# Hybrid gated-conv and forgetting-attention block: where four pairs of decay rows are issued, and when two rows of squares are taken

## The chip, the cores and the metric

The kernel runs on one core of one Trainium2 chip. The metric is the device time of one execution in microseconds, the median of several runs. TensorE is called PE here (its weight loads PEld), VectorE DVE, ScalarE ACT, GpSimd POOL and SyncE SP.

## The reference

One trunk layer over 512 positions of width 1024, all in float32, cut to what matters here:

```python
h = rms_norm(x, norm_mix_g)
cb, cc, cin, q, k, v, f_logit, g_logit = split(h @ w_in)
y_conv = (cb * causal_dwconv(cc * cin)) @ w_out_conv
F = cumsum(log_sigmoid(f_logit + b_f))                  # decay, one row per head
s = q.k / sqrt(64) + F[t] - F[s]                        # s <= t, 8 heads of 64
y_attn = softmax(s) @ v @ w_out_attn
x = x + (sigmoid(g_conv) * y_conv + sigmoid(g_attn) * y_attn) @ w_o
a, b = split(causal_dwconv(rms_norm(x, norm_ffn_g) @ w_up))   # 2 x 2816
x = x + (silu(a) * b) @ w_down
out = x * rsqrt(mean(x * x, -1) + 1e-6) * norm_f_g
```

## The kernel before

Everything is held transposed: features on the 128 partitions, the 512 positions along the free axis, so `x1` is eight rows of blocks (`x1[:, m, :]`, m = 0 to 7). Each float32 product is made of three matmuls on a high and a low half: a weight chunk arrives by DMA as `raw`, ACT copies it to the high half `wh` (L259), DVE subtracts to get the low half `wl` (L263), and PE multiplies high by high, low by high and high by low. This splitting is the work that PE always waits for, if it waits. The tiles `wh` and `wl` have two buffers each, `raw` has four (two to four for the forms below); SP issues the weight loads in the order of one list, `stream`, and each waits until the split has freed its buffer.

The program runs through stages: the projection of v, then q and k of the first two head pairs, then attention (32 units of one head and one block of 128 queries, with half a projection between two units as filler, L589 and L590 being the score matmuls), gates, mix, output projection, the up projection and the down projection.

**Decay rows.** The cumulated decay is in one tile `fr`, written once on DVE (L684). For every pair of heads `pr`, `evac_qk` evacuates q and k (`t_q`, `t_k`), copies and splits them on ACT (L531), POOL (L532) and DVE (L533), and `put_f` (L513) copies rows of `fr` by DMA into spare rows of the tiles `qb` and `kb`, two DMAs of 4 KB for q and two for k. Score matmul L590 multiplies `qb` by `kb` and so adds the decay. Pairs 0 and 1 use different `qb` and `kb` buffers; pairs 2 and 3 use them again. A score goes on to DVE (L594, minimum), ACT (L598, `pp`), POOL (L602, scaling) and back to PE, which transposes it (L618, `tp`) three units later.

**Down projection.** The function `seven` makes 2 by 2 blocks of it with seven products in place of eight. Its weights come as two chunks for each step, a plain one (`P`, three products for each block) and a formed one (`F`, four; sums of weights prepared in DRAM). Output rows are made in pairs i = 0 to 3, rows 2i and 2i + 1. In the second of the two phases pair 2 ends first, then pair 0, and then pair 1; pair 3's rows come at the very end by plain products. When a pair is done, `combine` puts its remaining additions (`z1` to `a4`, L1107 to L1126) into a list `later`; in phase 1 it adds two calls of `final_square` for the pair's two rows, which square a row on ACT (L1139 or L1142), add it to `ssq3` on DVE (L1143) and scale the row by the last norm's weight on ACT (L1144).

Work in `later` is done behind a weight split: `run_later(k, us)` goes through the list in order, takes each entry that is allowed from split `k` on while a budget of microseconds lasts, and stops at the first allowed entry that does not fit. The first number of an entry is the split from which it is allowed:

```python
if later[n][0] <= k and later[n][1] <= us + 0.1:
    us -= later[n][1]
    with after_split():
        later.pop(n)[3]()
elif later[n][0] <= k:
    return
```

PE's order is fixed by hand (`keep`). ACT, DVE and POOL orders outside `keep` come from the tile scheduler, which may move an instruction ahead of another.

Of the kernel before, what the change touches and what calls it, by code (L numbers as in the profile page):

```python
# [61 lines left out]
DOUBLES = GATES + STEPS[0] + STEPS[1]  # L62
# [4 lines left out]
def block_kernel(ctx, tc, xT, vecs, wv, win, wmix, wo, wup, wst, wdp, outT):  # L67
# [3 lines left out]
    nc = tc.nc  # L71
# [12 lines left out]
    def ring(*ids):  # L84
        st = [0]

        def f(name):
            st[0] += 1
            return bank(ids[(st[0] - 1) % len(ids)], name)

        return f
# [29 lines left out]
    stream = [(f"v{kb}", wv[kb], S + H) for kb in range(KB)]  # L121
# [247 lines left out]
    def ct(name):  # L369
        return ap.tile([P, S], F32, tag="ct", name=name, bufs=NCT)  # L370
# [109 lines left out]
    def proj(idx, name, evac, bank):  # L480
        st = {}

        def half(i):
            if i == 0:
                st["w"] = chunk(f"in{idx}")
                st["p"] = bank(f"p_{name}")
            wh, wl = st["w"]
            for kb in range(4 * i, 4 * i + 4):
                ks = slice(kb * P, (kb + 1) * P)
                mm3(st["p"], wh[:, ks], wl[:, ks], xgh[:, kb, :], xgl[:, kb, :], kb == 0, kb == KB - 1)  # L490
            if i == 1:

                while len(parts) < chunk.n + 2:
                    split()
                with after_split():
                    evac(st["p"])

        return [lambda: half(0), lambda: half(1)]
# [13 lines left out]
    def put_f(dst, f0, eng):  # L512
        eng.dma_start(dst.bitcast(F32), fr[f0 : f0 + H + 1 : H, :].bitcast(F32))  # L513

    def evac_qk(pr, isq):
        def f(p):
            nm = f"{'q' if isq else 'k'}{pr}"
            t = ct(f"t_{nm}")
            if isq:
                nc.vector.scalar_tensor_tensor(t, p, -(HD ** -0.5), rb1, op0=ALU.mult, op1=ALU.mult)  # L520
            else:
                nc.vector.tensor_mul(t, p, rb1)
            a = ap.tile([P, 2, S], F32R, tag="qt" if isq else "ka", name=f"a_{nm}", bufs=2)
            b = (QB if isq else KBt)[pr % 2]
            (QT if isq else KA)[pr] = a
            af = a.bitcast(F32)
            for e in range(2):
                own, other = slice(e * HD, (e + 1) * HD), slice((1 - e) * HD, (2 - e) * HD)
                second = (b[own, e, :], a[other, e, :])
                cp2, lo = second if isq else second[::-1]  # L530
                nc.scalar.activation(a[own, e, :], t[own, :], AF.Copy)  # L531
                nc.gpsimd.tensor_scalar(cp2, t[own, :], 1.0, 0.0, op0=ALU.mult, op1=ALU.add)  # L532
                nc.vector.tensor_sub(lo, t[own, :], af[own, e, :])  # L533
                f0 = 2 * pr + e + (2 * H if isq else 0)
                r = AUX[e] + (0 if isq else 2)
                put_f(b[r : r + 2, e, :], f0, nc.scalar if pr < 2 else nc.gpsimd)

        return f

# [127 lines left out]
    z, e, o = (ap.tile([n, S], F32, tag="pp", name=nm, bufs=NPP) for nm in ("fz", "fe", "fo"))  # L667
# [38 lines left out]
    f0, f1 = proj(12, "q0", st.append, ring(7))  # L706
# [21 lines left out]
    for idx in late:  # L728
        kind, i = divmod(idx, 4)
# [9 lines left out]
    for i in range(n + LA):  # L739
# [8 lines left out]
        if 0 <= i - LA < n:  # L748
            pr, e, qb = units[i - LA]
# [95 lines left out]
    def x_sums(qs):  # L845
        b11, b12, b21, b22 = (xq[:, qs, i, :] for i in range(4))

        def f():
            nc.vector.tensor_sub(b11, b11, b12)
            nc.vector.tensor_sub(b12, b22, b12)  # L850

        def g():
            nc.vector.scalar_tensor_tensor(b22, b11, -1.0, b22, op0=ALU.mult, op1=ALU.subtract)
            nc.vector.scalar_tensor_tensor(b21, b22, -1.0, b21, op0=ALU.mult, op1=ALU.subtract)

        return f, g
# [9 lines left out]
    for q in (0, 2):  # L866
        f, g = x_sums(slice(q, q + 2))
# [56 lines left out]
    for j in range(KB):  # L924
# [20 lines left out]
        a, b = gs  # L945
# [153 lines left out]
    def combine(ph, i, banks, ids):  # L1099

        m1, m2 = x1[:, 2 * i, :], x1[:, 2 * i + 1, :]
        p23, p45, p16, p7 = banks[0], banks[1], banks[2], banks[3][:, th[0]]
        t = {}

        def z1():
            t["z"] = fp.tile([P, S], F32, tag="fz", name=f"cz{ph}{i}", bufs=2)
            nc.scalar.activation(t["z"][:, th[0]], p16[:, th[0]], AF.Copy)  # L1107
            nc.vector.tensor_add(t["z"][:, th[1]], p16[:, th[1]], t["z"][:, th[0]])

        def a1():  # L1110
            nc.vector.tensor_add(m1, p23, m1)

        def u3():
            t["u"] = fp.tile([P, S], F32, tag="fz", name=f"cu{ph}{i}", bufs=2)[:, : 2 * P]
            nc.vector.tensor_add(t["u"], p7, t["z"][:, th[1]])
            nc.vector.tensor_add(m1[:, th[1]], p45[:, th[1]], m1[:, th[1]])

        def a2():
            nc.vector.tensor_sub(m2, m2, p45)

        def a3():
            nc.vector.tensor_add(m1, m1, t["z"])

        def a4():
            m2h = m2.rearrange(halves_of, h=2)
            nc.vector.tensor_sub(m2h, m2h, t["u"].unsqueeze(1).to_broadcast([P, 2, 2 * P]))  # L1126

        for f, us, x in ((z1, 0.42, 2), (a1, 0.7, 0), (u3, 0.85, 3), (a2, 0.7, 1), (a3, 0.7, None), (a4, 0.7, None)):
            later.append((0, us, () if x is None else ids if x == 3 else (ids[x],), f))
        if ph == 1:  # L1130
            first = [c[0] for c in stream].index(f"F{len(DOUBLES) - 2}") if i == 0 else 0
            for m in (2 * i, 2 * i + 1):
                later.append((first, 0.8, (), lambda m=m: final_square(m)))

    def final_square(m):
        y = x1[:, m, :]
        if final_square.first:
            final_square.first = False
            nc.scalar.activation(ssq3, y, AF.Square)  # L1139
        else:  # L1140
            sq = fp.tile([P, S], F32, tag="fu", name=f"sq3_{m}", bufs=3)
            nc.scalar.activation(sq, y, AF.Square)  # L1142
            nc.vector.tensor_add(ssq3, ssq3, sq)  # L1143
        nc.scalar.activation(y, y, AF.Copy, scale=col(GF + m))  # L1144
# [3 lines left out]
    for ph, (j0, j1) in enumerate(PHASES):  # L1148
        if ph:
            flush()  # L1150
            acc = ring(*X)
        if ph:
            make_forms(len(GATES) + len(STEPS[0]), len(DOUBLES), ph)
        for j in range(j0, j1):
            pu = None
            if j == 0:
                nrm = {}

                def mid():
                    nrm["c"] = rstd_col([ssq2], NT, 6, "n2")  # L1160

                def late():
                    nrm["b"] = rstd_sb(rstd_bc(nrm["c"], NT, 7, "n2"), "n2")

                pu = lead(["up0", "up1"], x1h, x1l, mid, late)
            glu(ph, j, up(j, nrm["b"], pu))
        assert not todo_bg
        seven(
            STEPS[ph], len(GATES) + ph * len(STEPS[0]), ({0: X, 1: Y, 3: X, 2: Y}, {0: X, 1: Y, 2: Y})[ph],
            lambda q, g: (gh[:, place(ph, q) + g, :], gl[:, place(ph, q) + g, :]),  # L1170
            goes_on=HELD if ph == 1 else None, stays=HELD if ph == 0 else None,
            done=lambda i, banks, ids: combine(ph, i, banks, ids),
        )
# [190 lines left out]
```

## Time and profile before

| | |
|---|---|
| median of 3 runs | 701.56 us (701.47 to 701.98) |
| profiled execution | 702.08 us |
| its span | 700.0 us |
| mean granted PE clock | 0.997 |
| PE busy | 690.9 us, 99% of the span |
| DVE, ACT, POOL busy | 501.7, 344.0, 171.5 us |

The profiled execution is 0.52 us above the median and 2.08 us longer than its span, which runs from the first to the last instruction. In rows of a timeline the first number is the start in us from the span's start, the second the length (of the whole group for "x2"), and the brackets hold the idle time before it and what ended it. ACTq, SPq and POOLq are an engine's queue issuing a DMA. Consecutive matmuls overlap: their start to start is what counts, not the length of one.

### The profile page before, as it was taken

What the parts mean: (1) busy time and instruction counts of PE and PEld (TensorE: products, weight loads), DVE (VectorE), ACT (ScalarE), POOL (GpSimd) and SP (SyncE); (2) the same over time, 40 slices, a digit from 0 to 9 for tenths busy, and PEclk for the clock granted to TensorE, in tenths of its full rate; (3) what the DMA queues carried; (4) which work ended last, traced back from release to release, by engine and by line L of the source; (5) the groups of instructions that cost most, each with busy time, mean ns of one, the idle gap of its engine ahead of it and who ended that gap; (6) DMA issues with size and microseconds to landing.
All of it is one profiled execution on the core that took longest, in us unless ns stands there. A gap on an engine that the chain in (4) does not pass through costs nothing. (4 is left out here: it accounts for less than half of the span.)

```text
span 700.0 us, 14606 instructions
## 1 busy us (share of the span) xinstructions
PE 690.9 (99%) x6008; PEld 689.2 (98%) x6008; DVE 501.7 (72%) x783; ACT 344.0 (49%) x546; POOL 171.5 (24%) x187
## 2 busy tenths in 40 slices
PE   9999999999999999999999999999999999999996
PEld 9999999999999999999999999999999999999995
DVE  6678877776678778754377777778774677877783
ACT  5574655645565444543344444445443345545563
POOL 4124846532100000224504214110000322311001
PEclk9999999999999999999999999999999999999998
DMA  7527978542452555586977855545546686676413
GB/s 251 155 85 255 210 186 196 124 91 89 149 172 80 179 185 178 182 298 150 216 192 169 218 121 129 157 159 176 194 132 223 146 190 158 182 185 166 147 31 121
DMA packets 52578, 116.02 MB, mean 166 GB/s; under 512 B 4848, under 2 KB 23296, under 8 KB 52512
## 3 DMA queue, kind: packets, MB, share of 16 engines
q1 hardware_dynamic: 37456, 94.16, 41.3%
q0 software_dynamic: 13792, 19.72, 17.4%
q10 hardware_dynamic: 1264, 1.22, 0.5%
q8 instruction: 47, 0.77, 0.4%
q14 instruction: 19, 0.16, 0.1%
HBM read 112.92 MB, written 33.03 MB: 208 GB/s over the span
## 5 line engine op out<-in xcount | busy, mean ns | idle before, releaser
L290 PE MATMUL p_up<-x1h,wh_up 128*128 128x256 f32 x536 | 104.5, 276 | 0.0
L290 PE MATMUL p_up<-x1h,wl_up 128*128 128x256 f32 x536 | 104.4, 276 | 0.0
L290 PE MATMUL p_up<-x1l,wh_up 128*128 128x256 f32 x536 | 104.3, 276 | 0.0
L259 ACT ACTIVATE wh_up<-raw_up 128x1024 fp32r<-128x1024 f32 x44 | 46.7, 1060 | 86.8 <-PE p_up L290 73.4
L290 PEld LDWEIGHTS p_up<-x1h,wl_up 128*128 128x128 f32 x536 | 80.7, 188 | 0.0
L290 PEld LDWEIGHTS p_up<-x1h,wh_up 128*128 128x128 f32 x536 | 80.7, 188 | 0.0
L290 PEld LDWEIGHTS p_up<-x1l,wh_up 128*128 128x128 f32 x536 | 80.6, 188 | 0.0
L263 DVE TENSOR_TENSOR wl_up<-raw_up,wh_up 128x1024 fp32r<-128x1024 f32 x44 | 53.8, 1223 | 20.6 <-ACT wh_up L259 20.6
L290 PE MATMUL p_in<-xgh,wl_in 128*128 128x256 f32 x288 | 56.7, 278 | 0.1
L290 PE MATMUL p_in<-xgh,wh_in 128*128 128x256 f32 x288 | 56.8, 279 | 0.0
L1061 POOL TENSOR_TENSOR ge<-fu,fu 128x512 f32<-128x512 f32 x11 | 17.1, 1550 | 161.6 <-DVE fu L547 150.9
L290 PE MATMUL p_in<-xgl,wh_in 128*128 128x256 f32 x288 | 56.5, 278 | 0.0
L201 POOL DMA_DIRECT2D f<-in_wst_dram x48 | 55.9, 1285 | 0.0
L1046 DVE TENSOR_TENSOR fz<-p_up,rb_n 128x512 f32<-128x512 f32 x44 | 30.3, 690 | 31.6 <-PE p_up L290 31.6
L263 DVE TENSOR_TENSOR wl_F<-raw_F,wh_F 128x1024 fp32r<-128x1024 f32 (+1 forms) x30 | 40.4, 1346 | 14.3 <-ACT wh_F L259 14.3
L259 ACT ACTIVATE wh_F<-raw_F 128x1024 fp32r<-128x1024 f32 (+1 forms) x30 | 31.5, 1051 | 28.8 <-PE dn L308 25.8
L290 PEld LDWEIGHTS p_in<-xgh,wh_in 128*128 128x128 f32 x288 | 44.7, 188 | 0.7
L290 PEld LDWEIGHTS p_in<-xgh,wl_in 128*128 128x128 f32 x288 | 43.6, 188 | 0.3 <-DVE wl_in L263 0.3
L290 PEld LDWEIGHTS p_in<-xgl,wh_in 128*128 128x128 f32 x288 | 43.7, 188 | 0.0
L308 PE MATMUL p_up<-x1h,wh_up 128*128 128x256 f32 x168 | 40.3, 277 | 0.0
L308 PE MATMUL p_up<-x1l,wh_up 128*128 128x256 f32 x168 | 40.2, 276 | 0.0
L263 DVE TENSOR_TENSOR wl_in<-raw_in,wh_in 128x1024 fp32r<-128x1024 f32 x26 | 34.6, 1332 | 7.1 <-ACT wh_in L259 6.9
(318 smaller groups left out, 2038.4 us busy)
## 6 DMA issues: line engine op xcount, KB each, us to landing
raw_up<-in_wup_dram SPq DMA_DIRECT2D x44, 512.0 KB, 4.9
raw_F<-f SPq DMA_DIRECT2D x29, 512.0 KB, 4.0
raw_in<-in_win_dram SPq DMA_DIRECT2D x26, 512.0 KB, 3.6
raw_P<-in_wst_dram SPq DMA_DIRECT2D x29, 384.0 KB, 3.7
f<-in_wst_dram POOLq DMA_DIRECT2D x29, 256.0 KB, 5.6
f<-in_wst_dram SPq DMA_DIRECT2D x14, 512.0 KB, 5.8
f<-in_wst_dram POOLq DMA_DIRECT2D x14, 512.0 KB, 8.0
f<-f SPq DMA_DIRECT2D x28, 256.0 KB, 5.0
```

Source lines behind the costliest of these rows:

```text
L201: return lambda: keep(nc.gpsimd.dma_start(dst, src, accum_op=ALU.add))
L259: ins = nc.scalar.activation(hi, raw, AF.Copy)
L263: ins = nc.vector.tensor_sub(lo, raw, hi.bitcast(F32))
L290: keep(nc.tensor.matmul(out[:, cs], w, x[:, cs], start=start and i == 0 and c == 0, stop=stop and i == 2 and c == len(cut) - 1,))
L308: keep(nc.tensor.matmul(out, wl if x == 1 else wh, xl if x == 2 else xh, start=opens and bk not in seen, stop=closes and bk not in left,))
L1046: nc.vector.tensor_mul(z, p, rb2)
L1061: keep(nc.gpsimd.tensor_mul(ge, a.rearrange(halves_of, h=2), b.rearrange(halves_of, h=2)))
```

## The change

Two edits. In `evac_qk` the DMAs of the decay rows get other queues: before, pairs 0 and 1 were on ACT and pairs 2 and 3 on POOL; now pair 0's q is on ACT, pair 0's k on SP, and pairs 1, 2 and 3 on POOL. In `combine` the two `final_square` calls of pair 2 are allowed only from the split of the last but one `F` chunk on, as those of pair 0 were before; those of pair 1 are allowed at once, as before.

```diff
@@ evac_qk
                 r = AUX[e] + (0 if isq else 2)
-                put_f(b[r : r + 2, e, :], f0, nc.scalar if pr < 2 else nc.gpsimd)
+                put_f(b[r : r + 2, e, :], f0, nc.gpsimd if pr else nc.scalar if isq else nc.sync)
@@ combine
         if ph == 1:
-            first = [c[0] for c in stream].index(f"F{len(DOUBLES) - 2}") if i == 0 else 0
+            first = [c[0] for c in stream].index(f"F{len(DOUBLES) - 2}") if i != 1 else 0
             for m in (2 * i, 2 * i + 1):
                 later.append((first, 0.8, (), lambda m=m: final_square(m)))
```

In the rows below a name ends in its buffer's number; `-` is before, `+` after. On ACT, where q and k of the first two pairs are evacuated (`qb_109` and `kb_111` are pair 0's, `qb_110` and `kb_112` pair 1's; `wh_in_708` is the first attention filler's weight):

```order
 L531 ACTIVATE a_k_648<-t_k_646 64x512 x2
 L513 DMA qb_109<-fr 2x512 x2
-L513 DMA kb_111<-fr 2x512 x2
 L259 ACTIVATE wh_in_708<-raw_in_453 128x1024
-L513 DMA qb_110<-fr 2x512 x2
+L531 ACTIVATE a_q_714<-t_q_712 64x512 x2
 L259 ACTIVATE wh_in_774<-raw_in_556 128x1024
-L531 ACTIVATE a_q_714<-t_q_712 64x512 x2
-L513 DMA kb_112<-fr 2x512 x2
 L598 ACTIVATE pp_800,m_798<-s_795,m_798 128x128
```

Six of the eight DMAs leave ACT, and pair 1's copies of q (`a_q_714`) move ahead of one weight split. Two of the six go to SP, between the weight loads `raw_in_624` and `raw_in_706`; the four of pair 1 go to POOL:

```order
 L532 TENSOR_SCALAR a_k_648<-t_k_646 64x512 x2
+L513 DMA qb_110<-fr 2x512 x2
+L513 DMA kb_112<-fr 2x512 x2
 L532 TENSOR_SCALAR qb_110<-t_q_712 64x512 x2
 L532 TENSOR_SCALAR a_k_780<-t_k_778 64x512 x2
```

On POOL they stand behind pair 0's copies and ahead of pair 1's. On DVE, at the same place, the two subtractions of `a_q_714` (L533) move ahead of the first score's minimum (`s_795`) and of the split `wl_in_775`.

On ACT near the end of the down projection (`wh_F_8496` of before is `wh_F_8494` now, `wh_P_8527` is `wh_P_8524`; `cz` is pair 0's `z1`; the row ahead of these is the split `wh_P_8466` in both):

```order
+L1107 ACTIVATE cz_8470<-dn_8257 128x256
+L259 ACTIVATE wh_F_8494<-raw_F_8309 128x1024
 L1139 ACTIVATE ssq_4484<-x_3960 128x512
-L1142 ACTIVATE sq_5_8472<-x_3960 128x512
-L1144 ACTIVATE x_3960<-x_3960,vec 128x512 x2
-L259 ACTIVATE wh_F_8496<-raw_F_8309 128x1024
-L1107 ACTIVATE cz_8500<-dn_8257 128x256
-L259 ACTIVATE wh_P_8527<-raw_P_8337 128x768
+L1144 ACTIVATE x_3960<-x_3960,vec 128x512
+L259 ACTIVATE wh_P_8524<-raw_P_8337 128x768
+L1142 ACTIVATE sq_5_8528<-x_3960 128x512
+L1144 ACTIVATE x_3960<-x_3960,vec 128x512
```

The squares and scalings of pair 2 leave the place ahead of the formed weight's split; one row of them now stands between that split and the next plain one, the other behind that. On DVE pair 0's first two additions (L1108, L1111) move ahead of the formed weight's `wl`, and the addition of `sq_5` (L1143) behind the next plain weight's `wl`. PE's instructions and their order are the same.

## The prediction

> **What bounds the kernel now.** First the page's busy times, then who PE and its weight loads waited for:
>
> ```profile
> PE 690.9 (99%) x6008; PEld 689.2 (98%) x6008; DVE 501.7 (72%) x783; ACT 344.0 (49%) x546; POOL 171.5 (24%) x187
> ```
> ```profile
> PE dn L308 <- ACT wh_F L259: 0.9, 1, 0.9
> ```
> ```profile
> PEld p_in L290 <- DVE wl_in L263: 0.3, 1, 0.3
> ```
>
> PE is the bound and its instructions don't change, so only its holes can be won. Behind its start the view of waits lists these two by name: 0.9 us for a formed weight's split on ACT, 0.3 us for a filler weight's low half on DVE. The change touches just those two places. The timeline of PE gives what each costs from start to start:
>
> ```profile
> 653.53 0.84 PE L308 MATMUL dn<-gh,wl_P 128*128 128x256 f32 x6
> ...
> 658.97 0.28 PE L308 MATMUL dn<-gh,wh_F 128*128 128x256 f32 x1
> ...
> 665.63 0.84 PE L308 MATMUL dn<-gh,wl_P 128*128 128x256 f32 x6
> 667.35 0.38 PE L308 MATMUL dn<-gh,wh_F 128*128 128x256 f32 x1 [0.88 <-ACT wh_F L259]
> ...
> 672.40 0.28 PE L308 MATMUL dn<-gh,wh_F 128*128 128x256 f32 x1
> ```
>
> Six low products of a P chunk, 24 products of an F and 18 of the next P take 658.97 - 653.53 = 5.44 us undisturbed, 0.1133 us each. The same 48 products take 672.40 - 665.63 = 6.77 us around the wait: it costs 1.33 us. Of that 667.35 - (665.63 + 6 x 0.1133) = 1.04 us is the hole itself and 0.29 us a slower pace behind it, up to 672.40.
>
> ```profile
> 53.01 0.28 PE L589 MATMUL s<-a_k,a_q 128*128 128x256 f32 x1
> ...
> 53.25 0.40 PE L290 MATMUL p_in<-xgh,wh_in 128*128 128x256 f32 x2
> 53.78 0.51 PE L290 MATMUL p_in<-xgh,wl_in 128*128 128x256 f32 x2
> ...
> 56.41 0.28 PE L589 MATMUL s<-a_k,a_q 128*128 128x256 f32 x1
> ...
> 59.42 0.28 PE L589 MATMUL s<-a_k,a_q 128*128 128x256 f32 x1
> ```
>
> From the first score to the second 56.41 - 53.01 = 3.40 us, from the second to the third, with the same 26 matmuls, 3.01 us. The early wait costs 0.39 us.
>
> **The late edit: squares behind the split.** ACT before:
>
> ```profile
> 663.26 0.83 ACT L259 ACTIVATE wh_P<-raw_P 128x768 fp32r<-128x768 f32 x1
> 663.99 0.61 ACT L1139 ACTIVATE ssq<-x 128x512 f32<-128x512 f32 x1
> 664.51 0.62 ACT L1142 ACTIVATE sq<-x 128x512 f32<-128x512 f32 x1
> 665.03 1.32 ACT L1144 ACTIVATE x<-x,vec 128x512 f32<-128x512 f32 x2
> 666.26 1.04 ACT L259 ACTIVATE wh_F<-raw_F 128x1024 fp32r<-128x1024 f32 x1
> 667.21 0.36 ACT L1107 ACTIVATE cz<-dn 128x256 f32<-128x256 f32 x1
> ```
>
> PE wanted `wh_F` at 665.63 + 0.68 = 666.31 and its copy ended at 667.30. Four activations of pair 2 stood ahead of it for 666.26 - 663.99 = 2.27 us. Now one `cz` of 0.36 us stands there: `wh_F` starts near 664.36 and ends near 665.40, 0.9 us ahead of PE. Its other wait, PE's last use of the buffer (the F before, whose high products are over by 664.0), isn't later.
>
> What is late next? On DVE, L1108 and L1111 now stand ahead of `wl_F`:
>
> ```profile
> 667.33 1.22 DVE L263 TENSOR_TENSOR wl_F<-raw_F,wh_F 128x1024 fp32r<-128x1024 f32 x1 [1.48 <-ACT wh_F L259]
> 668.48 0.42 DVE L1108 TENSOR_TENSOR cz<-dn,cz 128x256 f32<-128x256 f32 x1
> ...
> 669.68 0.68 DVE L1111 TENSOR_TENSOR x<-dn,x 128x512 f32<-128x512 f32 x1
> ```
>
> DVE had been free since 667.33 - 1.48 = 665.85. With these two, 1.10 us, and even with the addition of `sq_5` still counted, `wl_F` would start at 666.95 and end at 668.17; without that addition (0.68 by its like, L1111) at 667.49. PE wants it behind 16 high products, at 666.31 + 1.81 = 668.12. So it is in time by 0.6 us.
>
> The squares don't vanish. One square and one scaling (0.61 + 0.66 us) stand between `wh_F` and the next `wh_P`, which then ends near 665.40 + 1.27 + 0.83 = 667.50; PE wants it 24 products after 666.31, at 669.03: 1.5 us of cover. The other pair of activations ends near 668.8; the next `wh_F` waits for PE's high products of this F anyway, to 668.12 and a matmul's length, 668.40, and so ends at 668.8 + 1.04 = 669.84 against 671.07 wanted (666.31 + 42 x 0.1133): 1.2 us. If one of these covers failed, its excess would be PE's new wait.
>
> The gain passes on only if the end is PE's too:
>
> ```profile
> 683.83 0.43 DVE L1229 TENSOR_TENSOR ssq<-ssq,sq 128x256 f32<-128x256 f32 x1
> ```
> ```profile
> 684.40 0.58 PE L325 MATMUL pc_n<-ones,ssq 128*128 128x1 f32 x4
> ```
>
> DVE gave PE the first half's sum with about 0.14 us to spare (684.26 against 684.40). DVE's chain to there begins with the last weights' splits, which wait for PE to free buffers, so it moves with PE. I count the whole 1.33 us.
>
> By the row below the granted clock is full behind the hole, while the pace there is 0.1133 + 0.29 / 42 = 0.120 us:
>
> ```profile
> 667.00:669.00 2.00, 1.65 (x14) 1.00 0.05 18
> ```
>
> The Trainium skill ("TensorE: Matmul & The Clock Gate", Part 1) says the clock knows half and full rate only and falls after an idle window of about 3.4 us; by that a 1 us hole leaves the pace alone. The 1.00 agrees with it. If the slower pace then belonged to the stage and not to the hole, only the hole would come back: 1.04 for 1.33, and 700.13 in the end. I go by the rows, since the same kind and number of products ran at 0.1133 us up to 658.97.
>
> **The early edit: ACT's queue.**
>
> ```profile
> 48.32 1.17 ACTq L513 DMA_DIRECT2D qb<-fr  x1
> ...
> 50.13 1.17 ACTq L513 DMA_DIRECT2D kb<-fr  x2
> 51.41 1.06 ACT L259 ACTIVATE wh_in<-raw_in 128x1024 fp32r<-128x1024 f32 x1 [2.14 <-issue]
> ```
> ```profile
> 50.36 1.71 DVE L533 TENSOR_TENSOR kb<-t_k,a_k 64x512 fp32r<-64x512 f32 x2
> 52.50 1.23 DVE L263 TENSOR_TENSOR wl_in<-raw_in,wh_in 128x1024 fp32r<-128x1024 f32 x1 [0.43 <-ACT wh_in L259]
> ```
>
> The two `kb` issues hold the filler's split for 51.41 - 50.13 = 1.28 us. Without them `wh_in` ends near 51.2, and DVE's own work (to 52.07) is what `wl_in` waits for: it moves 0.43 us, from an end at 53.73 to 53.30. PE wants it two matmuls after 53.25, at 53.48. In time by 0.18 us, a thin margin: 0.39 us won, 0 at worst.
>
> Who waits behind the DMAs in their new places? SP's two wait for `fr`, which was there at 48.32 (the first issue), and hold the load behind them:
>
> ```profile
> 45.46 8.62 SPq L173 DMA_DIRECT2D raw_in<-in_win_dram  x2
> ```
> ```profile
> 65.68 1.06 ACT L259 ACTIVATE wh_in<-raw_in 128x1024 fp32r<-128x1024 f32 x1 [1.36 <-issue]
> ```
>
> That load is issued near 49.5 (48.32 and two issues at ACT's 0.58) in place of 45.46, 4 us late; its split is the fourth behind 50, at 65.68. Nothing.
>
> POOL's four stand ahead of pair 1's copies, and behind those the first scaled score, which PE transposes:
>
> ```profile
> 48.86 1.96 POOL L532 TENSOR_SCALAR a_k<-t_k 64x512 fp32r<-64x512 f32 x2
> 54.41 2.17 POOL L532 TENSOR_SCALAR qb<-t_q 64x512 fp32r<-64x512 f32 x2 [3.60 <-DVE t_q L520]
> ...
> 60.49 1.11 POOL L602 TENSOR_SCALAR pp<-pp,m 128x128 f32<-128x128 f32 x2
> ```
> ```profile
> L513 POOL DMA_DIRECT2D qb<-fr x4: 547/1440/2325, 73.5 to 108.5; - x4
> ```
> ```profile
> 65.44 0.27 PE L618 MATMUL tp<-ident,pp 128*128 128x128 f32 x1
> ```
>
> POOL sat idle for 3.60 us from 50.82. Four issues at the least price, 0.55, end at 53.0, inside that idle time. At the dearest, 2.33, they end at 60.1, the copies (2.17 + 1.96) at 64.3, the first `pp` (0.56) at 64.8; PE, 0.39 us earlier than now, wants it at 65.05. So between these prices the DMAs cost PE nothing. I take the least, since here POOL has nothing else to do. Pair 1's rows themselves are wanted eight units on. DVE's minimum of the first score now stands behind two subtractions (2.0 us later, about 56.5); its `pp` is then out of the bank near 57.4, and the third score, which uses the bank, comes at 59.42 - 0.39.
>
> Two rows bear on a rule here, a POOL issue and the DVE split that it overlaps:
>
> ```profile
> 94.56 1.07 POOL L201 DMA_DIRECT2D f<-in_wst_dram  x1
> ```
> ```profile
> 94.68 1.23 DVE L263 TENSOR_TENSOR wl_in<-raw_in,wh_in 128x1024 fp32r<-128x1024 f32 x1
> ```
>
> Neither is longer than elsewhere (`wl_in` above is 1.23 us with POOL idle). The Trainium skill ("SBUF — State Buffer", SBUF: two separate sides) warns that DVE work on the shared port can starve a DMA issued from POOL, and gives 620 ns alone and 3100 ns beside DVE. By that the four would take 12.4 us.
>
> **Sum.** 1.33 + 0.39 = 1.72 us off. The profiled 702.08 becomes 700.36, the median 701.56 becomes 699.84.
>
> **Rivals.** A measurement tells 0.2%, 1.40 us, from no change: below 700.16 is faster, above 702.96 slower.
>
> *Early wait stays* (0.10): the 0.18 us margin is eaten, DVE's `kb` subtractions or the first of POOL's issues being slower. For it: DVE, not ACT, becomes the releaser. 1.33 us off: 700.23.
>
> *The slow pace stays* (0.08): as above, 700.13.
>
> *Something late eats the gain* (0.08): DVE's `wl_F` (0.6 us of cover) or the sum at 684.40 (0.14) is late; half of the late gain goes, about 700.5.
>
> *POOL turns it round* (0.06): the issues are starved beside DVE. It decides from 2.4 us each, where `pp` meets 65.05; each further 0.1 costs 0.4 us; from 2.8 the whole gain is gone; at 3.2 `pp` is ready at 68.3, 3.26 us late: 701.56 - 1.72 + 3.26 = 703.1. Against it: the dearest row is 2.33, and the overlapped pair above. By the 3100 ns of the Trainium skill's page on SBUF it would be 702.7.
>
> The change not acting is excluded by the printed order. The forecast itself has 0.68; with the runs' spread of 0.5 us it ends below 700.16 in about 0.6, the two near-misses and the late one add 0.08. Slower by over the bound: 0.06, for POOL and what I have not seen. The range goes from 0.5 us under the forecast, the spread, to 701.0, where the first three rivals are in.
>
> **What would show it.** In the profile after: no wait of PE for `wh_F` and none of PEld for `wl_in`; the 48 products near 665 in 5.44 us; `wh_F` starting right behind `cz`; the first scores 3.01 us apart; POOL's four issues done before its `qb` copies. I am wrong if PE waits at 668 for `wl_F`, at a transpose near 65 for POOL, or if the holes close and the span doesn't shrink by their sum.

## The result and the profile after

The changed kernel took 700.12 us (median of 12 runs, 700.0 to 700.8) beside 701.81 us for the kernel before; the ratio is 0.9978, 95% interval 0.9969 to 0.9987. Timed once more it took 700.44 (700.01 to 700.71) beside 701.76, ratio 0.998 (0.9972 to 0.9988). The median of the 24 runs is 700.23. The forecast was 699.8, in the range 699.3 to 701.0.

The page of the changed kernel, its busy times:

```profile
PE 689.5 (99%) x6008; PEld 688.1 (99%) x6008; DVE 501.1 (72%) x783; ACT 344.4 (49%) x546; POOL 173.3 (25%) x191
```

The view of waits, PE and its weight loads, the whole list (us in total, times, longest):

```profile
PE warm L111 <- DVE ones L103: 1.0, 1, 1.0
PE pa L454 <- DVE wh_v L257: 0.4, 1, 0.4
PEld warm L111 <- DVE ones L103: 1.0, 1, 1.0
PEld pa L454 <- ACT ssq L421: 0.5, 1, 0.5
PEld dn L308 <- ACT wh_P L259: 0.3, 1, 0.3
```

The waits for `wh_F` and for `wl_in` are gone. What is left belongs to the start (L111, L454), but for the last row, a split of P just ahead of the late edit. The list of before doesn't have this row; its timeline has the stall all the same, a little shorter (the fourth row of the table below). The timeline of PE shows the three places:

```profile
52.47 0.28 PE L589 MATMUL s<-a_k,a_q 128*128 128x256 f32 x1
...
52.95 0.43 PE L290 MATMUL p_in<-xgh,wl_in 128*128 128x256 f32 x2
...
55.48 0.28 PE L589 MATMUL s<-a_k,a_q 128*128 128x256 f32 x1
...
662.69 0.62 PE L308 MATMUL dn<-gh,wl_F 128*128 128x256 f32 x4
...
664.87 0.84 PE L308 MATMUL dn<-gh,wl_P 128*128 128x256 f32 x6
665.55 0.28 PE L308 MATMUL dn<-gh,wh_F 128*128 128x256 f32 x1
...
670.31 0.28 PE L308 MATMUL dn<-gh,wh_F 128*128 128x256 f32 x1
```

The first two scores are 55.48 - 52.47 = 3.01 us apart, and the 48 products from 664.87 take 670.31 - 664.87 = 5.44 us, to the hundredth what the forecast has. The first half's sum, near the end, moved with PE: DVE again ends 0.14 us ahead of it (L1229 ends at 682.16, and L325 takes it at 682.30). ACT, POOL and DVE at the two places:

```profile
663.24 0.36 ACT L1107 ACTIVATE cz<-dn 128x256 f32<-128x256 f32 x1
663.50 1.05 ACT L259 ACTIVATE wh_F<-raw_F 128x1024 fp32r<-128x1024 f32 x1
...
665.73 0.83 ACT L259 ACTIVATE wh_P<-raw_P 128x768 fp32r<-128x768 f32 x1
...
667.75 1.05 ACT L259 ACTIVATE wh_F<-raw_F 128x1024 fp32r<-128x1024 f32 x1
```
```profile
50.36 1.15 POOL L513 DMA_DIRECT2D qb<-fr  x2
51.48 1.00 POOL L513 DMA_DIRECT2D kb<-fr  x2
53.50 1.78 POOL L532 TENSOR_SCALAR qb<-t_q 64x512 fp32r<-64x512 f32 x2 [1.02 <-DVE t_q L520]
```
```profile
49.84 1.71 DVE L533 TENSOR_TENSOR kb<-t_k,a_k 64x512 fp32r<-64x512 f32 x2
51.59 1.23 DVE L263 TENSOR_TENSOR wl_in<-raw_in,wh_in 128x1024 fp32r<-128x1024 f32 x1
```

`wh_F` starts right behind `cz` and ends at 664.55, 1.0 us ahead of PE (665.55). POOL's four issues take 0.53 us each beside DVE's subtractions, and POOL then still waits 1.02 us. `wl_in` ends at 52.82, 0.13 us ahead of PE (52.95).

Cut at five points, the profiled executions add up as follows (us; each entry is a difference of starts in the timeline of PE, the last one that between the last start and the execution's own time):

| stretch | before | changed | changed, second time | pair 1 on SP | `wx` later |
|---|---|---|---|---|---|
| to the first score | 53.01 | 52.47 | 53.04 | 52.47 | 52.47 |
| first to second score (early edit) | 3.40 | 3.01 | 2.99 | 2.99 | 3.01 |
| to the low products of the split ahead (`wl_F` x4) | 607.20 | 607.21 | 607.20 | 607.20 | 607.20 |
| to the six low products of P | 2.02 | 2.18 | 2.11 | 2.08 | 1.81 |
| the 48 products (late edit) | 6.77 | 5.44 | 5.46 | 5.43 | 5.44 |
| rest of the execution | 29.68 | 29.83 | 29.87 | 29.55 | 29.86 |
| time | 702.08 | 700.14 | 700.67 | 699.72 | 699.79 |

The second and the fifth row are the two edits: 1.72 us together. The first row differs by 0.6 us between two runs of the same kernel, so it isn't the change's; kernels with the early part of before reach the first score at 52.55 and 52.46 too (the first and the third experiment). The fourth row begins for before at this one:

```profile
663.61 0.62 PE L308 MATMUL dn<-gh,wl_F 128*128 128x256 f32 x4
```

Undisturbed, its 16 products would take 16 x 0.1133 = 1.81 us. So before lost 0.21 us there and the changed kernel 0.37 and 0.30. That difference can't be laid to the change: three experiments below that keep the late part of before took 2.06, 2.10 and 2.12 us. The fourth and the last row were not in the forecast's sum; the last two columns are experiments on them, below.

### The profile page after: what moved, and what is told of

Read it like the earlier page. It is cut to its first block, busy times and chain, and to the rows that moved or that the text cites. A ratio compares the mean times of both kernels' runs of the same rounds, so it can differ in the third digit from the quotient of the medians.

```text
span 697.9 us, 14608 instructions
## 1 busy us (share of the span) xinstructions
PE 689.5 (99%) x6008; PEld 688.1 (99%) x6008; DVE 501.1 (72%) x783; ACT 344.4 (49%) x546; POOL 173.3 (25%) x191
## 4 chain that ended last, share of the span: by engine, by line
PE 97%; DMA 1%; DVE 0%; SPq 0%; ACT 0%; issue 0%; DVEq 0%; ACTq 0%
PE p_up L290 26%; PE dn L308 20%; PE p_in L290 14%; PE p_up L308 8%; PE p_wo L290 6%; PE yc L290 3%; PE ya L290 3%; PE p_q L290 2%; PE p_k L290 2%; PE p_gb L290 2%; PE p_ga L290 2%; PE o L635 2%; PE pa L454 2%; PE pb L456 1%; PE tp L618 1%; PE pdB L290 1%
```

## The experiments

Theory: two independent waits are gone, worth 1.33 and 0.39 us, each by the part of the edit that stands beside it. Rivals: the parts need each other; the squares cost something where they went; one of the DMA moves is idle; the slow pace belongs to the stage and not to the hole.

**The late edit alone.** Against the changed kernel:

```diff
-                put_f(b[r : r + 2, e, :], f0, nc.gpsimd if pr else nc.scalar if isq else nc.sync)
+                put_f(b[r : r + 2, e, :], f0, nc.scalar if pr < 2 else nc.gpsimd)
```

> Only the squares of pair 2 are held back; the decay rows stay where they were. If the two edits act apart, PE's wait for wh_F is gone and the 48 products around it take 5.44 us in place of 6.77, so 1.33 us off (near 0.998 of before), while the first scores stay 3.40 us apart and PEld still waits 0.3 us for wl_in. If the slower pace behind the hole belonged to the stage and not to the hole, only 1.04 us would come back and the products would take 5.73 us. If the shorter span of the changed kernel came from its start, little would be seen in the time here.

Measured: 700.55 us beside 701.71, ratio 0.9986 (0.9977 to 0.9994). That is 1.16 us by the medians, a little under the 1.33 expected, which lies inside the interval. The view of waits still has:

```profile
PEld p_in L290 <- DVE wl_in L263: 0.4, 1, 0.4
```

The scores are 3.42 us apart, as before; there is no wait for `wh_F`, and the 48 products take 5.47 us.

**The early edit alone.**

```diff
-            first = [c[0] for c in stream].index(f"F{len(DOUBLES) - 2}") if i != 1 else 0
+            first = [c[0] for c in stream].index(f"F{len(DOUBLES) - 2}") if i == 0 else 0
```

> Only the decay rows are moved; the squares of pair 2 stay ahead of the formed weight. If the edits act apart, the first scores are 3.01 us apart in place of 3.40 and PEld does not wait for wl_in, while the 48 products near 665 us still take 6.77 us with a wait of 0.9 us for wh_F: 0.39 us off at most, 0.9994 of before, too little for the clock of the runs to tell from no change. If what is won early is lost again at the late waits (the P chunk's split hangs on a transfer), less than 0.39 us arrives at 663 us.

Measured: 701.35 us, ratio 0.9994 (0.9986 to 1.0003), so by time alone it can't be told from before. The trace can tell: the scores are 3.04 us apart and the late wait stands unchanged, with 6.78 us for the 48 products:

```profile
666.78 0.39 PE L308 MATMUL dn<-gh,wh_F 128*128 128x256 f32 x1 [0.88 <-ACT wh_F L259]
```

The two parts act apart and add. What the change brings comes mostly from the late edit.

**Without pair 2's squares.** The late edit was 'behind', not 'away'. To see whether the squares cost anything in their new place, this kernel has the early part of before and leaves out pair 2's squares, their addition to the sum and the final scaling of these two rows:

```diff
-            first = [c[0] for c in stream].index(f"F{len(DOUBLES) - 2}") if i != 1 else 0
-            for m in (2 * i, 2 * i + 1):
+            first = [c[0] for c in stream].index(f"F{len(DOUBLES) - 2}") if i == 0 else 0
+            for m in (() if i == 2 else (2 * i, 2 * i + 1)):
```

> The kernel before with the squares and the final scaling of pair 2's two rows left out altogether (the output lacks them). If moving them costs nothing, this wins the same as holding them back: the 48 products take 5.44 us, 1.33 us off and nothing more at the end. If they cost PE something in their new place, or DVE's chain to the last sums is the end, this is faster than the late edit alone by that amount, some tenths of a us.

Measured: 700.44 us, ratio 0.9984 (0.9974 to 0.9993), against 0.9986 for the late edit alone. ACT there:

```profile
665.45 0.85 ACT L259 ACTIVATE wh_P<-raw_P 128x768 fp32r<-128x768 f32 x1 [0.55 <-PE dn L308]
667.97 1.07 ACT L259 ACTIVATE wh_F<-raw_F 128x1024 fp32r<-128x1024 f32 x1 [1.67 <-PE dn L308]
```

Without the squares ACT waits for PE, 0.55 and 1.67 us: that is most of the room into which they were moved. What doesn't fit delays the two splits by some tenths of a microsecond, and PE doesn't want them yet. The 48 products take 5.46 us here and 5.47 with the late edit alone. Behind the split the squares cost PE nothing that these runs can tell.

**Which DMA move matters.** Only pair 0's k on SP (pair 1's four stay on ACT), and only pair 1's four on POOL (pair 0's four stay on ACT); the late wait is left in both:

```diff
-                put_f(b[r : r + 2, e, :], f0, nc.scalar if pr < 2 else nc.gpsimd)
+                put_f(b[r : r + 2, e, :], f0, nc.gpsimd if pr > 1 else nc.sync if pr == 0 and not isq else nc.scalar)
```
```diff
+                put_f(b[r : r + 2, e, :], f0, nc.gpsimd if pr else nc.scalar)
```

> The kernel before with pair 0's k rows issued on SP; pair 1's four DMAs stay on ACT, behind the filler's split. If the early wait comes from the two k issues ahead of that split, this edit alone removes it: wh_in starts 1.2 us earlier, wl_in right behind DVE's kb subtractions, and the first scores are 3.01 us apart. If the load of ACT's queue as a whole is what counts, the wait stays in part.

> The kernel before with pair 1's four DMAs issued on POOL; pair 0's k rows stay on ACT, ahead of the filler's split. If only what stands ahead of that split counts, nothing is won: the first scores stay 3.40 us apart and PEld waits 0.3 us for wl_in; POOL's four issues take 0.55 us each, in its idle time. If POOL's issues disturb DVE's splits, wl_in is longer than 1.23 us and PE waits longer than before.

Measured, one execution each: 700.7 and 702.0 us beside 701.35. Scores of the first, then of the second:

```profile
52.46 0.28 PE L589 MATMUL s<-a_k,a_q 128*128 128x256 f32 x1
55.50 0.28 PE L589 MATMUL s<-a_k,a_q 128*128 128x256 f32 x1
```
```profile
52.67 0.28 PE L589 MATMUL s<-a_k,a_q 128*128 128x256 f32 x1
56.08 0.28 PE L589 MATMUL s<-a_k,a_q 128*128 128x256 f32 x1
```

3.04 us with pair 0's two on SP, 3.41 with pair 1's four on POOL. The two issues that stand directly ahead of the split are the early wait, to 0.03 us; moving the four of pair 1 brings PE nothing.

**Holes of three lengths.** Is the slower pace behind the hole the hole's? The changed kernel with ACT's copy of three formed weights far ahead of the end repeated two, three and five times more, so that PE waits:

```diff
+HOLES = {"F12": 2, "F15": 3, "F18": 5}
...
+            for _ in range(HOLES.get(nm, 0)):
+                nc.scalar.activation(hi, raw, AF.Copy)
```

> The changed kernel with the high copy of three formed weights in the first phase of the down projection (F12, F15, F18, near 480 to 510 us) made 2, 3 and 5 times more, each copy 1.05 us, so that PE meets three holes of its own: with the 1.7 us that a split usually has in hand, near 0.4, 1.5 and 3.6 us. If a slower pace follows a hole, the matmuls behind each run at about 0.118 to 0.120 us for some 5 us in place of 0.1133, with a loss that does not grow much with the hole (0.2 to 0.3 us); if it was a thing of that place in the program, they run at 0.1133 at once. If a hole of over 3.4 us lets the clock fall to half, as the Trainium skill (TensorE: Matmul & The Clock Gate, Part 1) has it, the third is followed by a stretch at twice the spacing and a granted clock under 1.

Measured: 711.72 us in one execution. The holes came out longer than expected (0.4, 1.5 and 3.6 us), since ACT took other work between the copies. PE's timeline, the six low products ahead of each hole, the first product behind it, and for the last two the next F:

```profile
482.11 0.84 PE L311 MATMUL dn<-gh,wl_P 128*128 128x256 f32 x6
483.35 0.38 PE L311 MATMUL dn<-gh,wh_F 128*128 128x256 f32 x1 [0.40 <-ACT wh_F L262]
...
486.19 0.28 PE L311 MATMUL dn<-gh,wh_P 128*128 128x256 f32 x1
...
497.07 0.84 PE L311 MATMUL dn<-gh,wl_P 128*128 128x256 f32 x6
500.11 0.39 PE L311 MATMUL dn<-gh,wh_F 128*128 128x256 f32 x1 [2.19 <-ACT wh_F L262]
...
506.66 0.28 PE L311 MATMUL dn<-gh,wh_F 128*128 128x256 f32 x1
...
515.50 0.84 PE L311 MATMUL dn<-gh,wl_P 128*128 128x256 f32 x6
520.59 0.58 PE L311 MATMUL dn<-gh,wh_F 128*128 128x256 f32 x1 [4.25 <-ACT wh_F L262]
...
527.60 0.28 PE L311 MATMUL dn<-gh,wh_F 128*128 128x256 f32 x1
```

Against the undisturbed pace of 0.1133 us the first hole costs 486.19 - 482.11 - 30 x 0.1133 = 0.68 us, the second 506.66 - 497.07 - 5.44 = 4.15, the third 527.60 - 515.50 - 5.44 = 6.66. From start to start the holes themselves are 0.56, 2.36 and 4.41 us. So each costs more than its length, by 0.12, 1.79 and 2.25 us. For the two long ones the reason is the clock. The table by stretches (length, PE busy, granted clock in the fifth column, DMA):

```profile
501.00:502.00 1.00, 1.00 (x8) 0.63 0.00 0
...
504.00:505.00 1.00, 1.00 (x7) 0.66 0.96 276
...
518.00:520.00 2.00, 0.00 (x0) 0.58 0.00 0
...
525.00:526.00 1.00, 1.00 (x10) 0.92 0.80 324
```

The clock is halved from 501.26 to 504.68 and from 518.32 to 525.16 (worked out from the partial stretches: 0.63 of full speed in a microsecond is half speed for 0.74 of it). PE works in 3.42 us of the first time and, from 520.59 on, in 4.57 of the second; at half speed that loses 1.71 and 2.29 us, against 1.79 and 2.25 measured. The second hole was expected not to do this. A hole of 1 us, as before had it, stays below this. There the pace fell by some 6% only (0.120 us in the prediction), at a clock of 1.00. And that pace belongs to the hole: the same stage runs at 0.1133 us in the changed kernel and at 0.114 in the late edit alone. Behind the first of the three holes the 24 products take (486.19 - 483.35) / 24 = 0.118 us each, at a clock of 1.00. Its length varies, though. In the execution with pair 0's k on SP, whose hole was like that of before, it was soon over:

```profile
664.80 0.84 PE L308 MATMUL dn<-gh,wl_P 128*128 128x256 f32 x6
666.53 0.38 PE L308 MATMUL dn<-gh,wh_F 128*128 128x256 f32 x1 [0.88 <-ACT wh_F L259]
...
671.41 0.28 PE L308 MATMUL dn<-gh,wh_F 128*128 128x256 f32 x1
```

6.61 us for the 48, of which the hole is 1.05 and the slower pace 0.12, where it was 0.29 in the profile of before.

**The P chunk's split.** The wait of the weight loads for `wh_P` (0.3 us) lies 2 us ahead of the late edit. There ACT splits `wx`, a small weight for the end, ahead of `wh_P`, and waits for its transfer, first in the changed kernel, then in before:

```profile
661.96 0.63 ACT L259 ACTIVATE wx<-raw_dp 128x512 fp32r<-128x512 f32 x1 [1.27 <-DMA raw_dp<-in_wdp_dram]
662.50 0.83 ACT L259 ACTIVATE wh_P<-raw_P 128x768 fp32r<-128x768 f32 x1
```
```profile
662.72 0.64 ACT L259 ACTIVATE wx<-raw_dp 128x512 fp32r<-128x512 f32 x1 [1.10 <-DMA raw_dp<-in_wdp_dram]
```

The next kernel issues the split of `wx` behind the split of the formed weight (`mark[0]`):

```diff
-    fetch(1, [wx[:, a : a + 4 * P] for a in (80, 752)])
+    with tc.issue_after(mark[0]):
+        fetch(1, [wx[:, a : a + 4 * P] for a in (80, 752)])
```

> The changed kernel with the copy of the small plain weight chunk (wx) held behind the last but one formed weight's split, so that the P chunk's split ahead of it no longer stands behind a copy that waits for a transfer. In the changed kernel PE waits 0.24 us there, from 663.14 to 663.38, and starts 0.12 us slower. If that wait hangs on the transfer through ACT's order, it goes: 0.3 to 0.4 us off the changed kernel, near 699.8 us, and the chunk's later users are still in time (the third chunk's transfer then starts some 3 us later). If the P chunk's split is bound by PE's buffer instead, nothing changes; if the later chunk is late, PE waits at the plain products near 677 us.

Measured: 700.11 us, ratio 0.9973 (0.9965 to 0.9982), where 699.8 us was expected. As that interval overlaps the changed kernel's, both were then run on one chip, the kernel with `wx` later being the same as here:

> The changed kernel once more, on the same chip as the next run, so that the two can be set side by side. If the times vary only by the start-up (about 0.5 us from run to run), it lies at 699.9 to 700.4 with a ratio to before of 0.997 to 0.998.

> The changed kernel with ACT's split of the small weight wx put behind the split of wh_P. If the wait of the P chunk's split on the transfer of raw_dp costs what the traces show (0.2 to 0.4 us), it is faster than the changed kernel beside it by 0.2 to 0.4 us; if that wait is made good later, the two are equal within 0.1 us.

Measured: 700.44 (a little above what was expected) and 699.83 us, ratios to before 0.998 (0.9972 to 0.9988) and 0.9972 (0.9962 to 0.9981); the means are 700.39 and 700.01, one to the other 0.9994 (0.9991 to 0.9998, by drawing the runs anew). PE with `wx` later:

```profile
662.68 0.62 PE L311 MATMUL dn<-gh,wl_F 128*128 128x256 f32 x4
...
664.49 0.84 PE L311 MATMUL dn<-gh,wl_P 128*128 128x256 f32 x6
```

1.81 us are 16 products at 0.1133: the stall is gone. From the first score to the end of the execution it is 647.32 us, beside 647.67 and 647.63 in the two of the changed kernel, so the 0.3 to 0.4 us are kept to the end.

**What lies beyond the span.** An execution's time is longer than its span, and the difference is not the same in all kernels: 2.20 to 2.28 us in all 24 runs of the changed kernel, 2.19 to 2.28 with the early edit alone, but 1.89 to 2.14 with the late edit alone, and 2.0 on average (1.72 to 2.15) in runs of before. Only the early edit raises it; of its two moves, in one execution each, pair 1's four on POOL have 2.20 and pair 0's two on SP 1.80. Three kernels on one chip: the changed one with pair 1's four DMAs on SP in place of POOL, the same with `wx` later, and the changed one with pair 0's two k DMAs on POOL as well:

```diff
+                put_f(b[r : r + 2, e, :], f0, nc.gpsimd if pr > 1 else nc.scalar if isq and pr == 0 else nc.sync)
```
```diff
+                put_f(b[r : r + 2, e, :], f0, nc.gpsimd if pr or not isq else nc.scalar)
```

> Pair 1's four DMAs issued on SP, between weight loads, in place of POOL; the rest as changed. What an execution takes beyond its span was 2.23 us in the changed kernel's runs and 2.24 with the early edit alone, 2.01 with the late edit alone and 2.0 in those of before. If the DMAs that POOL issues more (12 of decay rows for 8) add that, here it is 2.0 again, at the changed kernel's span, and the time 0.2 us lower than the changed kernel's (near 700.0, ratio 0.9975). If it belongs to the freed ACT queue or to chance, it stays at 2.23.

> Pair 1 on SP and the split of wx behind the formed weight's. If both small losses add, the time beyond the span is 2.0 us and the P chunk's split takes 1.81 us: a time near 699.7, ratio near 0.997 or just under.

> Pair 0's two k DMAs on POOL too (14 of decay rows there, for 12 in the changed kernel and 8 before). If each POOL issue adds some 0.06 us beyond the span, that is 2.35 us here; if it is a step, it stays at 2.23. On POOL the six issues take about 3.2 us from 50.4 to 53.6 and delay qb's copies by 0.1 us, which hides; the first scores stay 3.01 us apart.

Measured: 699.84, 700.04 and 700.12 us, ratios 0.9977 (0.9967 to 0.9986), 0.9975 (0.9965 to 0.9985) and 0.9982 (0.9973 to 0.9991). Beyond the span: 1.97 to 2.04, 1.96 to 2.05 and 1.75 to 1.83 us. With pair 1 on SP it is as in before, and no run of it overlaps one of the changed kernel. So with pair 1's four issues on POOL an execution takes 0.23 us more beyond the span than with them on SP, and no wait in the trace shows it. The third kernel fits neither of the two values expected for it and refutes a price for each issue: with six more on POOL the time beyond the span falls. But its span has grown behind the same last instructions. The last DMA issues on ACT of the changed kernel, of pair 1 on SP and of all six on POOL:

```profile
692.57 0.98 ACTq L1241 DMA_DIRECT2D out_dram<-x  x2
```
```profile
692.44 0.98 ACTq L1241 DMA_DIRECT2D out_dram<-x  x2
```
```profile
692.47 0.98 ACTq L1241 DMA_DIRECT2D out_dram<-x  x2
```

From there to the end of the time it is 700.14 - 692.57 = 7.57, 699.72 - 692.44 = 7.28 and 699.97 - 692.47 = 7.50 us: the part behind the last work is longer by 0.2 to 0.3 us in the two kernels with pair 1 on POOL, wherever the span ends. The other profiled executions agree: counted in the same way, all eight with pair 1 on POOL have 7.50 to 7.60 us, and all six with it on ACT or SP 7.03 to 7.41 (before 7.41). What in that part takes it was not found out.

Pair 1 on SP with `wx` later has the lowest single run of all (699.53) and both stretches short (1.81 and 29.60 us), but its profiled execution reached the first score only at 53.03, and its median misses the 699.7 expected. By medians it can't be told from `wx` later alone or pair 1 on SP alone; each of the three is faster than before by its interval.

## Why the prediction was right

**The late edit** (1.33 us forecast) gave 1.33 and 1.31 us in two profiles. The covers held with more room than forecast: `wh_F` 1.0 us ahead (0.9), `wl_F` 1.0 (0.6; 666.38 by the row below against 665.55 + 1.81). From the rows of ACT above, the next `wh_P` ended at 666.56, 1.7 us ahead of PE (1.5), the next `wh_F` at 668.80, 1.5 ahead (1.2). DVE:

```profile
665.17 1.21 DVE L263 TENSOR_TENSOR wl_F<-raw_F,wh_F 128x1024 fp32r<-128x1024 f32 x1
```

The rival that the slow pace stays is out: both the hole and the pace came back. So is the rival of something late: DVE and ACT were both in time, and the view lists no wait of PE behind 664.87. The slower pace was a term of luck all the same, since it lasted 0.12 us in another execution with the same hole.

**The early edit** (0.39) gave 0.39 and 0.41. The margin of 0.18 us was 0.13. The rival that the early wait stays is out. The forecast had taken all six moves together. Pair 0's two alone bring 3.04 us.

**POOL** didn't turn it round: 0.53 us for each issue, the cheapest end of the forecast's range, beside 1.71 and 1.23 us of DVE work. The Trainium skill ("SBUF — State Buffer", SBUF: two separate sides) gives 3100 ns for a DMA issued from POOL that overlaps a DVE `tensor_copy`. Beside these subtractions nothing of it showed, neither in POOL's time nor in DVE's; a `tensor_copy` was not among them, so the figure itself is not tested here.

**Where the sum was incomplete.** The step that failed is "The profiled 702.08 becomes 700.36": it takes what lies around the two holes as constant. The two holes closed by 1.72 us, and yet the span shrank by 2.1 in the first profile and by 1.6 in the second, and the median by 1.69 and 1.32. One term of cost was missing, and two that vary from run to run. The four DMAs on POOL take 0.23 us beyond the span: the cost of POOL's issues was looked for in what waits behind them, and stood at the end of the program instead. The start-up varies: the first score comes between 52.46 and 53.30 us, and two executions of one kernel (`wx` later) lie 0.8 us apart. The split of P waits for a transfer and took 2.02 to 2.18 us in kernels that have `wx` in its old place, before among them. 1.72 less 0.23 is 1.49 us, in the middle between the two measured differences; with a start-up that varies by more than half a microsecond that is as near as this goes. That the first median came within 0.03 us of the forecast gain is luck in part. Pair 1 on SP, which doesn't have POOL's term, took 699.84 us beside 701.60, 1.76 us less.

## What to carry to other kernels

A wait on the bounding engine is priced by the distance between two of its own instructions, with and without the wait, and not by the idle time that the view names: 1.33 us stood behind a listed 0.9, and with longer holes 4.15 behind 2.19. Work that must be done sometime is put behind the split that the bounding engine waits for next, into the time in which the producer would wait for its buffers. And an edit that moves DMAs from one issuing engine to another is compared by the whole time too, since part of its cost can lie outside of everything that the trace shows as a wait.

## What the runs showed of the hardware

- Half clock behind a hole of 2.36 us: PE stood still for 2.36 us and was halved 1.15 us after it had started again, for 3.42 us; with 4.41 us it was halved 2.3 us before it started again, for 6.84 = 2 x 3.42 us. From the end of the first half-clock time to the start of the second it is 518.32 - 504.68 = 13.64 = 4 x 3.41 us. So the decision falls at fixed points 3.41 us apart, by what PE did in the time before; in the three such stretches that led to half clock (up to 501.26, 518.32 and 521.74 us) PE stood still for 2.0 to 2.3 us. The Trainium skill ("TensorE: Matmul & The Clock Gate", Part 1) has the same free-running window, 3413 ns, and full or half rate only, and this agrees; that a window must be idle to bring the clock down is more than these runs needed.
- Behind a hole of 1 us or less the matmuls come some 6% further apart for a while, at a granted clock of 1.00. It took 0.29 us in all in one execution and 0.12 in another with the same hole. Neither a wait nor the clock shows it; its cause is open.
- The time from the span's start to the first score varies from run to run: 52.47 and 53.04 us in two executions of the changed kernel, 53.30 and 52.47 in two with `wx` later.
